# The first pair of inner blocks of the SwiGLU: seven-product scheme against plain products by token halves

## Chip, cores and metric

The kernel runs on one core of one Trainium2 chip. The time is device microseconds (us) of one execution. Engines are named as in the profile: PE is TensorE (PEld its weight loads), DVE is VectorE, ACT is ScalarE, POOL is GpSimd, SP is the engine that issues most DMAs (SPq is its queue). L12 is line 12 of the kernel. All instructions that go through the kernel's recording wrapper carry line L195, so they are told apart here by the names of the tiles they write and read.

## What is computed

One inference step of a two-layer encoder on 576 tokens (512 prompt tokens and 64 of a sample), width 1024. In each layer three mixers, then a cross attention, then a SwiGLU; each adds to the residual `x`. Only the last part and the norm ahead of it matter here:

```python
x = x + mixers(rmsnorm(x, g_mix_norm))
x = x + memory_cross_attention(rmsnorm(x, g_cross_norm), mem_k, mem_v, w)
h = rmsnorm(x, g_ffn_norm)                            # 576 x 1024
x = x + (silu(h @ w_gate) * (h @ w_up)) @ w_down      # inner width 2816
```

## The kernel before

The residual lies transposed in the tile `X`: eight pieces `k` of 128 rows, 576 token columns, in two token halves `a` of HF = 288. Products are made in fp32r with each operand split into a rounded part H and a remainder L (`split_to`, L453: ACT copies H, DVE subtracts to get L), and three matmuls H·H, H·L, L·H per piece (`mm3`, L429). One such matmul is 128x128 by 128x288.

The inner width of 2816 is done in 11 blocks `p` of 256 columns. A block is a gate product and an up product (`gated`, L1658), each from a 1 MB weight slice fetched by SP. Each product is a 2x2 block product (two halves of the 1024 rows, two halves of the output columns, two token halves) that `winograd` (L606) makes with seven products of 12 matmuls where the plain way has eight. For this it needs sums of weight quarters (`wino_w`, L571: four DVE sums and the splits, tiles `sum`, `sH`, `sL`, `wH`, `wL`) and sums of activation quarters. Results come as pairs that ACT and DVE add up (`part` on ACT, then a DVE addition into `gate` or `u`).

The activation quarters come from `WNorm` (L514). `add` (L522) is called after each of the 16 additions into X at the end of cross attention; ACT copies X times the gain into `xs` and squares it, DVE sums the squares (tiles `u`). When a token half `a` is complete, `finish(a)` (L531) has PE sum the squares over rows by a matmul with `ones_x` into a bank T, ACT takes Ln and Exp of it, DVE scales `xs` by the result. For `a` = 0 the two quarters b11, b21 are split into `bH`, `bL`; these are the operands of products 1 and 2. For `a` = 1 DVE and ACT also make t1 = b12-b11, t2 = b22-t1, t3 = b22-b12, t4 = b21-t2 (tiles `tA`, `tB`) and split them and b22 into five tiles `bT`, the operands of products 3 to 7.

Products 1 and 2 of both gate and up of block 0 need nothing of the second token half. `gated` therefore starts gate (`next(g)`) and up (`next(h)`) of block 0 before it runs on with either. All engines' queues are in order; a scheduler sets the order by its own estimates from the order in the code and the data each instruction needs. PSUM banks are three rings, D and T of three and S of two. Raw weights have two slots (`wraw`), and the big tiles (`xs`, `bH`, `bT`, `actH` and others) eleven slots.

Of the kernel before, what the change touches and what calls it, by code (L numbers as in the profile page):

```python
# [25 lines left out]
HF = T // 2  # L26
# [190 lines left out]
def tile_hybrid(ctx, tc, ins, outs):  # L217
# [54 lines left out]
    def ps_(tag):  # L272
        return clock.tile(pp.tile([128, 512], F32, tag=tag, name=nm(tag), bufs=PB[tag]), tag, PB[tag])
# [27 lines left out]
    def tt(out, a, b, op, eng=None):  # L301
        (eng or nc.vector).tensor_tensor(out, a, b, op=op)
# [95 lines left out]
    def load_w(src, kt, n, src2=None, by="m"):  # L398
        return split_w(fetch_w(src, kt, n, src2), by)
# [114 lines left out]
    class WNorm:  # L514
# [16 lines left out]
        def finish(self, a):  # L531

            r = u()[:, 0:HF]
            rstd_bcast(self.acc[a], ones_x, r)
            n = 4 * HF
            b11, b21, b12, b22 = (self.x[i][:, q * n:(q + 1) * n] for i in range(2) for q in range(2))

            def scaled(x):
                x = x.rearrange("p (k t) -> p k t", t=HF)
                tt(x, x, r.unsqueeze(1).broadcast_to([128, 4, HF]), MUL)  # L540

            if a == 0:
# [12 lines left out]
            tt(t2, b22, t1, SUB)
            split_to(t2, Ha[:, n:2 * n], La[:, n:2 * n])
            split_to(t1, Ha[:, 0:n], La[:, 0:n])
            tt(t3, b22, b12, SUB)
            split_to(t3, Hb[:, 0:n], Lb[:, 0:n])
            tt(t4, b21, t2, SUB)  # L560
            split_to(t4, Hb[:, n:2 * n], Lb[:, n:2 * n])
            split_to(b22, Q[:, 0:n], Q[:, n:2 * n])
            self.p.update({5: (Ha, La, 0), 6: (Ha, La, 1), 7: (Hb, Lb, 0), 4: (Hb, Lb, 1), 3: (Q, Q, 0)})

        def part(self, p, i, k):

# [331 lines left out]
    def layer(l, xn):  # L898
# [759 lines left out]
        def gated(p, aH, aL, k0):  # L1658

            cs = lambda a: slice(a * HF, (a + 1) * HF)  # L1660
            done, done2 = [0, 0], [0, 0]
            s = [u("gate") for _ in range(2)]

            def gate(m, a, d, c):
                tt(s[m][:, cs(a)], d, c, ADD)
                done[m] += 1
                if done[m] == 2:
                    act(s[m], s[m], AF.Silu)

# [12 lines left out]

            h = winograd(wino_w(I["w_up"][l, :, p * 256:(p + 1) * 256]), xf, up_)
            next(h)
            if not p:

                run(g)
            run(h)
# [84 lines left out]
```

## Time and profile before

| | |
|---|---|
| median of 3 runs | 1718.99 us (1717.65 to 1723.28) |
| profiled execution, its own time | 1715.83 us |
| its span, first to last instruction | 1714.1 us |
| mean granted TensorE clock | 0.990 of full speed |
| busy: PE, PEld, DVE, ACT, POOL | 96%, 89%, 72%, 53%, 12% |

The busy shares are means over the whole span. A PE instruction counts as busy also while its clock is granted at half rate, so the granted clock and the number of instructions in a stretch are read beside them. Times below are counted from the span's start. The SwiGLU of layer 0 begins at 459 us, that of layer 1 at about 1303.6 us.

### The profile page before, as it was taken

To read this page: it belongs to the slowest core of one execution; us is meant where nothing else is said; L and a number is where in the kernel's file an instruction comes from. 1 tells how busy PE (TensorE), PEld (TensorE's weight loads), DVE (VectorE), ACT (ScalarE), POOL (GpSimd) and SP (SyncE) were. 2 spreads that over 40 slices of the span, in tenths; PEclk is the share of its full clock that TensorE was granted. 3 is DMA by queue.
4 is the path that set the end of the run, shared out by engine and by line. 5 is a ranking of instruction groups with operands and counts; after the bars stand their busy time and mean duration, and the time that the engine had idled before them with its cause. 6 is when DMAs were issued, how large, how long until landed. Compare 5 with 4: busy or idle time off the path is not lost.

```text
span 1714.1 us, 30856 instructions
## 1 busy us (share of the span) xinstructions
PE 1650.6 (96%) x12231; PEld 1532.3 (89%) x12231; DVE 1231.7 (72%) x2496; ACT 904.7 (53%) x1929; POOL 206.7 (12%) x303
## 2 busy tenths in 40 slices
PE   8999989999899999999999989999997999999998
PEld 8887887789889999999998978877897999999998
DVE  5737798776898677766557378987668986766763
ACT  6426678655654444344443456876567544334431
POOL 4323341020000000000134042400200000000000
PEclk9999999999999999999999999999999999999999
DMA  5321230022022323322222213200211233233221
GB/s 165 112 72 58 68 112 26 26 74 75 25 75 98 99 75 98 95 81 96 79 84 84 85 43 105 74 26 25 99 50 50 75 99 99 74 99 99 78 96 56
DMA packets 113647, 133.30 MB, mean 78 GB/s; under 512 B 10610, under 2 KB 95712, under 8 KB 113504
## 3 DMA queue, kind: packets, MB, share of 16 engines
q1 hardware_dynamic: 113120, 131.30, 24.1%
q8 instruction: 96, 1.57, 0.4%
q14 instruction: 47, 0.39, 0.1%
q0 software_dynamic: 352, 0.03, 0.0%
q10 hardware_dynamic: 32, 0.01, 0.0%
HBM read 123.64 MB, written 7.68 MB: 77 GB/s over the span
## 4 chain that ended last, share of the span: by engine, by line
PE 75%; DVE 13%; ACT 4%; issue 3%; POOL 2%; DMA 1%; POOLq 0%; ACTq 0%; DVEq 0%; SPq 0%
PE ffn0.D L195 9%; PE ffn1.D L195 8%; PE ffn0.S L195 6%; PE ffn0.T L195 6%; PE ffn1.S L195 6%; PE ffn1.T L195 6%; PE win1.D L195 4%; PE win0.D L195 4%; PE cross1.D L195 3%; PE cross0.D L195 3%; PE wout1.D L195 2%; PE wout0.D L195 2%; PE cross1.T L195 1%; PE cross0.T L195 1%; PE mlap1.T L195 1%
## 5 line engine op out<-in xcount | busy, mean ns | idle before, releaser
L195 ACT ACTIVATE ffn1.wH<-ffn1.wraw 128x1024 fp32r<-128x1024 f32 x66 | 60.6, 918 | 115.7 <-PE ffn1.T L195 61.4
L195 ACT ACTIVATE ffn0.wH<-ffn0.wraw 128x1024 fp32r<-128x1024 f32 x66 | 60.6, 918 | 111.0 <-PE ffn0.T L195 60.8
L195 DVE TENSOR_TENSOR ffn0.sL<-ffn0.sum,ffn0.sH 128x1024 fp32r<-128x1024 f32 x44 | 53.8, 1222 | 41.1 <-ACT ffn0.sH L195 41.1
L195 DVE TENSOR_TENSOR ffn1.sL<-ffn1.sum,ffn1.sH 128x1024 fp32r<-128x1024 f32 x44 | 53.8, 1222 | 40.4 <-ACT ffn1.sH L195 40.4
L195 PE MATMUL ffn0.D<-cross0.bT,ffn0.sH 128*128 128x288 f32 x352 | 73.9, 301 | 1.5 <-ACT ffn0.sH L195 0.7
L195 PE MATMUL ffn1.D<-cross1.bT,ffn1.sH 128*128 128x288 f32 x352 | 72.8, 297 | 2.2 <-ACT cross1.bT L195 1.2
L195 DVE TENSOR_TENSOR ffn1.wL<-ffn1.wraw,ffn1.wH 128x1024 fp32r<-128x1024 f32 x66 | 68.8, 1044 | 7.8 <-ACT ffn1.wH L195 7.2
L195 DVE TENSOR_TENSOR ffn0.wL<-ffn0.wraw,ffn0.wH 128x1024 fp32r<-128x1024 f32 x66 | 68.8, 1044 | 7.8 <-ACT ffn0.wH L195 7.2
L195 PE MATMUL ffn1.S<-cross1.bT,ffn1.sH 128*128 128x288 f32 x352 | 72.9, 298 | 1.3 <-ACT cross1.bT L195 0.6
L195 PE MATMUL ffn0.S<-cross0.bT,ffn0.sH 128*128 128x288 f32 x352 | 72.9, 298 | 0.7 <-ACT cross0.bT L195 0.5
L195 POOL TENSOR_TENSOR ffn0.u<-ffn0.u,ffn0.u 128x576 f32<-128x576 f32 x6 | 10.0, 1665 | 470.5 <-DVE ffn0.wL L195 463.5
L195 PEld LDWEIGHTS ffn0.D<-cross0.bT,ffn0.sH 128*128 128x128 f32 x352 | 57.6, 192 | 3.7 <-ACT ffn0.part L195 1.2
L195 ACT ACTIVATE ffn0.sH<-ffn0.sum 128x1024 fp32r<-128x1024 f32 x44 | 46.3, 1055 | 27.6 <-PE ffn0.S L195 22.8
L195 ACT ACTIVATE ffn1.sH<-ffn1.sum 128x1024 fp32r<-128x1024 f32 x44 | 46.3, 1055 | 27.4 <-PE ffn1.S L195 23.1
L195 PEld LDWEIGHTS ffn1.D<-cross1.bT,ffn1.sH 128*128 128x128 f32 x352 | 57.1, 190 | 3.6 <-ACT cross1.bT L195 1.4
L195 PEld LDWEIGHTS ffn1.S<-cross1.bT,ffn1.sH 128*128 128x128 f32 x352 | 57.8, 192 | 2.0 <-ACT cross1.bT L195 0.9
L195 PEld LDWEIGHTS ffn0.S<-cross0.bT,ffn0.sH 128*128 128x128 f32 x352 | 57.8, 192 | 1.5 <-ACT cross0.bT L195 0.8
L195 PE MATMUL ffn0.D<-cross0.bT,ffn0.sL 128*128 128x288 f32 x176 | 52.9, 301 | 0.0
L195 PE MATMUL ffn0.S<-cross0.bT,ffn0.sL 128*128 128x288 f32 x176 | 52.8, 300 | 0.0
L195 PE MATMUL ffn1.S<-cross1.bT,ffn1.sL 128*128 128x288 f32 x176 | 52.7, 299 | 0.0
L195 PE MATMUL ffn1.D<-cross1.bT,ffn1.sL 128*128 128x288 f32 x176 | 52.5, 298 | 0.0
L195 ACT ACTIVATE ffn0.part<-ffn0.D 128x288 f32<-128x288 f32 x66 | 26.9, 407 | 41.4 <-PE ffn0.D L195 41.4
(903 smaller groups left out, 6453.9 us busy)
## 6 DMA issues: line engine op xcount, KB each, us to landing
ffn0.wraw<-in_w_gate_dram SPq DMA_DIRECT2D x11, 1024.0 KB, 5.3
ffn0.wraw<-in_w_up_dram SPq DMA_DIRECT2D x11, 1024.0 KB, 5.3
ffn0.wraw<-in_w_down_dram SPq DMA_DIRECT2D x11, 1024.0 KB, 5.0
ffn1.wraw<-in_w_gate_dram SPq DMA_DIRECT2D x11, 1024.0 KB, 5.3
ffn1.wraw<-in_w_up_dram SPq DMA_DIRECT2D x11, 1024.0 KB, 5.4
ffn1.wraw<-in_w_down_dram SPq DMA_DIRECT2D x11, 1024.0 KB, 5.1
win1.wraw<-in_w_in_dram SPq DMA_DIRECT2D x7, 1024.0 KB, 5.4
win0.wraw<-in_w_in_dram SPq DMA_DIRECT2D x6, 1024.0 KB, 5.6
```

The source lines that it names most:

```text
L195: r = fn(*args, **kw)
```

## The change

`finish(1)` only scales and splits the two quarters b12 and b22 (tiles `bQ`, called P and Q below). The four sums move into a method of their own, `sums`, which uses one tile instead of two for them. Block 0 is no longer done by `gated` but by `first`: gate and up as plain products, all of token half 0 (from `bH`, `bL`), then `sums`, then all of token half 1 (from P and Q). Silu reads the PSUM bank directly, and so does the multiplication by it. No weight sums are made for this block. Blocks 1 to 10 stay as they were, without the interleaving.

```diff
@@ WNorm.finish, from L545 @@
                 self.p = {1: (H, L, 0), 2: (H, L, 1)}
+                self.sides = [[(H, L, 0), (H, L, 1)]]
                 return
-            ta, tb = big(name="tA"), big(name="tB")
-            t1, t2, t3, t4 = ta[:, 0:n], ta[:, n:2 * n], tb[:, 0:n], tb[:, n:2 * n]
-            Ha, La, Hb, Lb, Q = (big(F32R, "bT") for _ in range(5))
-            scaled(b12)
-            tt(t1, b12, b11, SUB)
-            scaled(b22)
-            tt(t2, b22, t1, SUB)
-            split_to(t2, Ha[:, n:2 * n], La[:, n:2 * n])
-            split_to(t1, Ha[:, 0:n], La[:, 0:n])
-            tt(t3, b22, b12, SUB)
-            split_to(t3, Hb[:, 0:n], Lb[:, 0:n])
-            tt(t4, b21, t2, SUB)
-            split_to(t4, Hb[:, n:2 * n], Lb[:, n:2 * n])
-            split_to(b22, Q[:, 0:n], Q[:, n:2 * n])
-            self.p.update({5: (Ha, La, 0), 6: (Ha, La, 1), 7: (Hb, Lb, 0), 4: (Hb, Lb, 1), 3: (Q, Q, 0)})
+            P, Q = big(F32R, "bQ"), big(F32R, "bQ")
+            for x, y in ((b12, P), (b22, Q)):
+                scaled(x)
+                split_to(x, y[:, 0:n], y[:, n:2 * n])
+            self.p[3] = (Q, Q, 0)
+            self.sides.append([(P, P, 0), (Q, Q, 0)])
+
+        def sums(self):
...
+            t = big(name="tA")
+            x, y = t[:, 0:n], t[:, n:2 * n]
+            Ha, La, Hb, Lb = (big(F32R, "bT") for _ in range(4))
+            tt(x, b12, b11, SUB)
+            tt(y, b22, x, SUB)
+            split_to(y, Ha[:, n:2 * n], La[:, n:2 * n])
+            split_to(x, Ha[:, 0:n], La[:, 0:n])
+            tt(x, b22, b12, SUB)
+            split_to(x, Hb[:, 0:n], Lb[:, 0:n])
+            tt(y, b21, y, SUB)
+            split_to(y, Hb[:, n:2 * n], Lb[:, n:2 * n])
...
@@ gated, from L1670 @@
-            g = winograd(wino_w(I["w_gate"][l, :, p * 256:(p + 1) * 256]), xf, gate)
-            next(g)
-            if p:
-                run(g)
+            run(winograd(wino_w(I["w_gate"][l, :, p * 256:(p + 1) * 256]), xf, gate))
...
+        def first(aH, aL):
+
+            ws = [load_w(I["w_gate"][l, :, 0:256], KD, 256), None]
+            raw = fetch_w(I["w_up"][l, :, 0:256], KD, 256)
...
+            s, t = [u("gate") for _ in range(2)], [u() for _ in range(2)]
+            n = 0
+            for a in range(2):
+                cs = slice(a * HF, (a + 1) * HF)
+                for w, up_ in zip(ws, (False, True)):
+                    for m in range(2):
+                        d = ps_("DTS"[n % 3])[:, 0:HF]
+                        n += 1
+                        for k in range(KD):
+                            mm3(d, w[0](k, m * 128, m * 128 + 128), w[1](k, m * 128, m * 128 + 128),
+                                xf.plain(a, 0, k), xf.plain(a, 1, k), k == 0, k == KD - 1)
+                        if up_:
+                            tt(t[m][:, cs], d, s[m][:, cs], MUL)
+                        else:
+                            act(s[m][:, cs], d, AF.Silu)
+                        if up_ and a:
+                            split_to(t[m], aH[:, m, :], aL[:, m, :])
+                if not a:
+                    xf.sums()
...
-                gated(p0 + i, aH, aL, 2 * i)
+                if p0 + i:
+                    gated(p0 + i, aH, aL, 2 * i)
+                else:
+                    first(aH, aL)
```

PE's queue of layer 0 around the matmul with `ones_x` for the second token half (T_5585), before:

```order
L195 MATMUL ffn0.D_5699<-cross0.bL_5482,ffn0.wH_5677 128x288
L195 MATMUL ffn0.D_5699<-cross0.bH_5481,ffn0.wL_5678 128x288
L195 MATMUL cross0.T_5585<-cross0.u_5581,ones_x 128x288
L195 MATMUL ffn0.T_5659<-cross0.bH_5481,ffn0.wH_5622 128x288
L195 MATMUL ffn0.T_5659<-cross0.bL_5482,ffn0.wH_5622 128x288
```

and now (S_5680 is an up product of half 0, T_5654 a gate product of half 0):

```order
L195 MATMUL ffn0.S_5680<-cross0.bL_5482,ffn0.sH_5615 128x288
L195 MATMUL ffn0.S_5680<-cross0.bH_5481,ffn0.sL_5616 128x288
L195 MATMUL cross0.T_5585<-cross0.u_5581,ones_x 128x288
L195 MATMUL ffn0.T_5654<-cross0.bH_5481,ffn0.wH_5609 128x288
L195 MATMUL ffn0.T_5654<-cross0.bL_5482,ffn0.wH_5609 128x288
```

Before, 24 matmuls of the SwiGLU stand ahead of T_5585 and 24 that need only the first half behind it; now 46 stand ahead and 50 behind. After those 50 come the 96 of half 1, which read `bQ`.

DVE's queue of layer 0 from the scaling of the second token half on, before:

```order
L195 TENSOR_TENSOR cross0.xs_4717<-cross0.xs_4717,cross0.u_5584 128x1152 x2
L195 TENSOR_TENSOR cross0.tA_5589<-cross0.xs_4717,cross0.xs_4716 128x1152
L195 TENSOR_TENSOR ffn0.gate_5618<-ffn0.T_5659,ffn0.part_5657 128x288
L195 TENSOR_TENSOR cross0.tA_5589<-cross0.xs_4717,cross0.tA_5589 128x1152
L195 TENSOR_TENSOR ffn0.wL_5696<-ffn0.wraw_5675,ffn0.wH_5695 128x512
L195 TENSOR_TENSOR cross0.bT_5592<-cross0.tA_5589,cross0.bT_5591 128x1152 x2
```

and now:

```order
L195 TENSOR_TENSOR cross0.xs_4717<-cross0.xs_4717,cross0.u_5584 128x1152 x2
L195 TENSOR_TENSOR cross0.bQ_5589<-cross0.xs_4717,cross0.bQ_5589 128x1152
L195 TENSOR_TENSOR ffn0.u_5625<-ffn0.S_5680,ffn0.gate_5623 128x288
L195 TENSOR_TENSOR cross0.bQ_5590<-cross0.xs_4717,cross0.bQ_5590 128x1152
L195 TENSOR_TENSOR ffn0.tA_5732<-cross0.xs_4717,cross0.xs_4716 128x1152
L195 TENSOR_TENSOR ffn0.u_5626<-ffn0.D_5706,ffn0.gate_5624 128x288
L195 TENSOR_TENSOR ffn0.tA_5732<-cross0.xs_4717,ffn0.tA_5732 128x1152
L195 TENSOR_TENSOR ffn0.bT_5734<-ffn0.tA_5732,ffn0.bT_5733 128x1152 x2
```

The remainders of P and Q now come ahead of the sums, which follow them.

DVE's queue of layer 0 during the last additions into X of the first token half, before (`wraw_5675` is the up weight of block 0):

```order
L195 TENSOR_TENSOR ffn0.wL_5641<-ffn0.wraw_5620,ffn0.wH_5640 128x512
L195 TENSOR_TENSOR X<-X,cross0.D_5404 128x288
L195 TENSOR_TENSOR cross0.u_5401<-cross0.u_5401,cross0.u_5383 128x288
L195 TENSOR_TENSOR ffn0.sum_5681<-ffn0.wraw_5675 128x512
L195 TENSOR_TENSOR X<-X,cross0.D_5422 128x288
```

and now (`wraw_5861` is the gate weight of block 1, whose DMA takes the slot of block 0's up weight):

```order
L195 TENSOR_TENSOR ffn0.wL_5610<-ffn0.wraw_5603,ffn0.wH_5609 128x1024
L195 TENSOR_TENSOR cross0.u_5401<-cross0.u_5401,cross0.u_5383 128x288
L195 TENSOR_TENSOR X<-X,cross0.D_5404 128x288
L195 TENSOR_TENSOR ffn0.sum_5867<-ffn0.wraw_5861 128x512
L195 TENSOR_TENSOR X<-X,cross0.D_5422 128x288
```

The first reader of the third 1 MB weight slice of the SwiGLU now stands ahead of the addition D_5422 and all later ones into X; before, it was the first reader of the second slice.

## Rows read from the trace of the kernel before

**Rows 1.** Page, part 1: busy us, share of span, instructions.

```profile
PE 1650.6 (96%) x12231; PEld 1532.3 (89%) x12231; DVE 1231.7 (72%) x2496; ACT 904.7 (53%) x1929; POOL 206.7 (12%) x303
```

**Rows 2.** Chain of waits within 620 to 626: start us, us, what.

```profile
622.67 3.19 PE ffn0.D L195 x24
```

**Rows 3.** Windows of 62 us: length, busy us (xinstructions) per engine, PE clock, DMA.

```profile
458.00:520.00 62.00, 54.29 (x353) 51.16 (x352) 54.56 (x73) 37.82 (x58) 0.00 (x0) 0.92 0.21 69
520.00:582.00 62.00, 62.00 (x470) 62.00 (x469) 51.67 (x83) 28.70 (x41) 0.00 (x0) 1.00 0.27 86
1302.50:1364.50 62.00, 52.90 (x353) 49.80 (x352) 54.72 (x73) 37.93 (x58) 0.00 (x0) 0.94 0.21 69
1364.50:1426.50 62.00, 62.00 (x470) 62.00 (x469) 51.58 (x83) 28.90 (x41) 0.00 (x0) 1.00 0.27 86
```

**Rows 4.** Waits of PE, 458 to 496: waited for, us in total, times, longest.

```profile
PE cross0.T L195 <- DVE cross0.u L195: 3.3, 1, 3.3
...
PE ffn0.D L195 <- DVE cross0.bL L195: 0.9, 1, 0.9
...
PE ffn0.D L195 <- ACT cross0.bH L195: 0.3, 1, 0.3
PE ffn0.T L195 <- ACT cross0.bT L195: 0.3, 1, 0.3
```

**Rows 5.** Windows, shorter, the start of layer 0's SwiGLU (columns as in rows 3).

```profile
458.00:464.00 6.00, 4.48 (x30) 3.78 (x28) 6.00 (x10) 5.91 (x13) 0.00 (x0) 1.00 0.01 3
...
467.00:471.00 4.00, 4.00 (x19) 3.90 (x20) 2.34 (x2) 2.87 (x4) 0.00 (x0) 0.62 0.00 0
...
474.00:482.00 8.00, 6.64 (x24) 5.77 (x24) 7.19 (x7) 3.25 (x4) 0.00 (x0) 0.57 0.42 131
```

**Rows 6.** Timeline of PE: start us, us, instruction, shapes [idle before, releaser].

```profile
459.01 0.53 PE L195 MATMUL ffn0.D<-cross0.bH,ffn0.wH 128*128 128x288 f32 x2 [0.25 <-ACT cross0.bH L195]
460.40 0.40 PE L195 MATMUL ffn0.D<-cross0.bL,ffn0.wH 128*128 128x288 f32 x1 [0.86 <-DVE cross0.bL L195]
...
466.86 0.75 PE L195 MATMUL cross0.T<-cross0.u,ones_x 128*128 128x288 f32 x2 [3.26 <-DVE cross0.u L195]
...
468.95 0.45 PE L195 MATMUL ffn0.T<-cross0.bH,ffn0.wL 128*128 128x288 f32 x1
469.19 0.45 PE L195 MATMUL ffn0.T<-cross0.bH,ffn0.wH 128*128 128x288 f32 x1
```

**Rows 7.** Timeline of ACT, 457 to 474.

```profile
457.79 1.17 ACT L195 ACTIVATE cross0.bH<-cross0.xs 128x1152 fp32r<-128x1152 f32 x1 [0.86 <-DVE cross0.xs L195]
...
462.29 0.39 ACT L195 ACTIVATE ffn0.part<-ffn0.D 128x288 f32<-128x288 f32 x1
...
463.63 0.41 ACT L195 ACTIVATE ffn0.part<-ffn0.D 128x288 f32<-128x288 f32 x1
...
468.18 0.45 ACT L195 ACTIVATE cross0.u<-cross0.u 128x288 f32<-128x288 f32 x1
468.64 1.28 ACT L195 ACT_TABLE_LOAD   x1
469.94 0.63 ACT L195 ACTIVATE ffn0.wH<-ffn0.wraw 128x512 fp32r<-128x512 f32 x1
```

**Rows 8.** Timeline of DVE, 455 to 488.

```profile
466.34 0.46 DVE L195 TENSOR_TENSOR cross0.u<-cross0.u,cross0.u 128x288 f32<-128x288 f32 x1 [0.30 <-ACT cross0.u L195]
468.66 2.63 DVE L195 TENSOR_TENSOR cross0.xs<-cross0.xs,cross0.u 128x1152 f32<-128x1152 f32 x2 [1.86 <-ACT cross0.u L195]
471.20 1.35 DVE L195 TENSOR_TENSOR cross0.tA<-cross0.xs,cross0.xs 128x1152 f32<-128x1152 f32 x1
...
474.10 0.68 DVE L195 TENSOR_TENSOR ffn0.wL<-ffn0.wraw,ffn0.wH 128x512 fp32r<-128x512 f32 x1
...
482.40 1.23 DVE L195 TENSOR_TENSOR ffn0.sL<-ffn0.sum,ffn0.sH 128x1024 fp32r<-128x1024 f32 x1 [1.22 <-ACT ffn0.sH L195]
```

**Rows 9.** Page, part 6: DMA issues, KB each, median us from issue to landing.

```profile
ffn0.wraw<-in_w_gate_dram SPq DMA_DIRECT2D x11, 1024.0 KB, 5.3
```

More of the change, by code (lines that the diff above doesn't have):

```diff
@@ L547, in finish, with plain @@
                 self.p = {1: (H, L, 0), 2: (H, L, 1)}
+                self.sides = [[(H, L, 0), (H, L, 1)]]
                 return
-            ta, tb = big(name="tA"), big(name="tB")
-            t1, t2, t3, t4 = ta[:, 0:n], ta[:, n:2 * n], tb[:, 0:n], tb[:, n:2 * n]
-            Ha, La, Hb, Lb, Q = (big(F32R, "bT") for _ in range(5))
-            scaled(b12)
-            tt(t1, b12, b11, SUB)
-            scaled(b22)
-            tt(t2, b22, t1, SUB)
-            split_to(t2, Ha[:, n:2 * n], La[:, n:2 * n])
-            split_to(t1, Ha[:, 0:n], La[:, 0:n])
-            tt(t3, b22, b12, SUB)
-            split_to(t3, Hb[:, 0:n], Lb[:, 0:n])
-            tt(t4, b21, t2, SUB)
-            split_to(t4, Hb[:, n:2 * n], Lb[:, n:2 * n])
-            split_to(b22, Q[:, 0:n], Q[:, n:2 * n])
-            self.p.update({5: (Ha, La, 0), 6: (Ha, La, 1), 7: (Hb, Lb, 0), 4: (Hb, Lb, 1), 3: (Q, Q, 0)})
+            P, Q = big(F32R, "bQ"), big(F32R, "bQ")
[5 more added lines that the diff above has]
+        def sums(self):
+            n = 4 * HF
+            b11, b21, b12, b22 = (self.x[i][:, q * n:(q + 1) * n] for i in range(2) for q in range(2))
+            t = big(name="tA")
[9 more added lines that the diff above has]
+            split_to(y, Hb[:, n:2 * n], Lb[:, n:2 * n])
+            self.p.update({5: (Ha, La, 0), 6: (Ha, La, 1), 7: (Hb, Lb, 0), 4: (Hb, Lb, 1)})
+        def plain(self, a, i, k):
+            t = self.sides[a][k // 4]
+            c = ((t[2] + (i if t[0] is t[1] else 0)) * 4 + k % 4) * HF
+            return t[i][:, c:c + HF]
         def part(self, p, i, k):
@@ L1681, in up_ @@
                     split_to(t[m], aH[:, k0 + m, :], aL[:, k0 + m, :])
[L1683 to L1688, printed above, removed]
+            run(winograd(wino_w(I["w_up"][l, :, p * 256:(p + 1) * 256]), xf, up_))
+        def first(aH, aL):
+            ws = [load_w(I["w_gate"][l, :, 0:256], KD, 256), None]
+            raw = fetch_w(I["w_up"][l, :, 0:256], KD, 256)
+            parts = []
+            for m in range(2):
+                H, L = (clock.tile(turn["pool"].tile([128, 1024], F32R, tag=tag, name=nm(tag), bufs=2), tag, 2)
+                        .rearrange("p (k n) -> p k n", n=128) for tag in ("sH", "sL"))
+                split_to(raw[:, :, m * 128:(m + 1) * 128], H, L)
+                parts.append((H, L))
+            ws[1] = [lambda k, c0, c1, i=i: parts[c0 // 128][i][:, k, :] for i in range(2)]
+            s, t = [u("gate") for _ in range(2)], [u() for _ in range(2)]
[3 more added lines that the diff above has]
+                for w, up_ in zip(ws, (False, True)):
+                    for m in range(2):
+                        d = ps_("DTS"[n % 3])[:, 0:HF]
[11 more added lines that the diff above has]
+                    xf.sums()
         def down(gi, p0, kt, aH, aL):
```

## The prediction

> **What bounds the kernel now.** The page's first part comes first: PE is busy 96% of the span [rows 1], so the change can only win where PE stands or runs slowly. The chain of waits gives PE's pace in the SwiGLU: 24 matmuls of 288 columns in 3.19 us, 0.133 us each [rows 2]. The windows view then shows where this pace is missed. A stretch of 62 us in the middle of the SwiGLU holds 470 PE instructions; the 62 us around its start hold 353, in both layers alike [rows 3]. That is 117 x 0.133 = 15.6 us lost per layer, 31.1 in both, and all of it lies in the stretch that the change rewrites.
>
> The loss has two sources. PE waits eight times, from 3.3 us down to 0.3 [rows 4]. The longest wait is for the sum of squares of the second token half: everything that could run on the first half alone and stood ahead of the matmul with ones_x is used up, and that matmul blocks PE's queue until 466.86 [rows 6]. The later waits are for the sums' H and L parts (bT). The second source is the clock: 1.00 while PE worked up to 464, then a granted 0.62 and 0.57 of full speed in stretches behind the long wait [rows 5]; between 468.95 and 469.19 one matmul takes 0.24 us, the 1.2 GHz level in place of 2.4 [rows 6].
>
> **The change, part by part** (times are layer 0's; layer 1 has the same rows and the same loss).
>
> Added work: eight products for seven, 12 more matmuls for gate and 12 for up. 24 x 0.133 = 3.2 us per layer, on PE, with nothing to hide them: 6.4 us in all.
>
> The long wait. 46 matmuls now stand ahead of the ones_x matmul, three of them before L of the first half is there. From 460.40 [rows 6] the other 43 take 5.7 us, to 466.1. Its input is the last sum of squares, at 466.34 + 0.46 = 466.8 before [rows 8]. ACT's queue paces that sum, and the two part copies of 0.39 and 0.41 us that stood in it [rows 7] are gone, so it comes 0.7 us sooner (both overlap their neighbours a little), at 466.1. The wait goes from 3.3 us to between 0 and 0.7 (0.7 if the copies did not matter); I take 0.2, since the two ends meet.
>
> Does half 1 find its operands? PE: the ones_x matmul takes 0.75 [rows 6], then 50 matmuls of half 0 take 6.7, so half 1 is reached at 473.6. ACT and DVE, all 0.7 earlier than before: Exp, that ended at 468.63 [rows 7], ends at 467.9; the table load of 1.28 to 469.2; Silu of the first gate product, priced as the part copy, 0.4, to 469.6; the H copy of P, as the bH copy, 1.17 [rows 7], to 470.8. DVE scales in 2.63 [rows 8] from 467.95, so the first quarter is there in time and DVE is free at 470.6; L of P takes 1.35, to 472.2. Then on ACT a second Silu and H of Q, to 472.4, on DVE a multiplication of 0.46 and L of Q, to 474.0. PE wants L of P at 473.6 and Q twelve matmuls later, at 475.2. Both are ready, with 1.4 and 1.2 us to spare. I take no wait here; past that slack, a delay costs its own length.
>
> The table load is the one step in that chain that could be longer than its row: 1.28 us, with the next ACT instruction 0.02 us after its end [rows 7]. The Trainium skill (ScalarE: Activation LUTs, What ACT_TABLE_LOAD costs) adds a drain of about 1.38 us to each switch, 2.66 in all; by that P and Q would come 1.4 us later, use up the slack just found and leave up to 0.2 us of wait per layer, 0.4 in the sum. The row shows no such gap, so the sum above goes by the row.
>
> The sums now run on DVE while PE works through half 1, 96 matmuls or 12.8 us, to 486.4; block 1's first two products need only the first half and last 24 matmuls more, to 489.6. DVE from 474.0: four subtractions and four remainders at 1.35, a weight remainder of 0.68, two multiplications of 0.46 and the first weight-sum remainder of 1.23 [rows 8], 13.6 us, plus one H copy of 1.17 that DVE must await: 488.8 if nothing overlaps. Neighbours overlap by nearly 0.1 us each, so about 488. PE wants it at 489.6; slack 1 us or somewhat more. Before, the sums ended at about the same time, but with PE waiting for them. I take no wait here either.
>
> What stays. The wait of 0.3 and 0.9 us for bH and bL [rows 4], and the ones_x matmul, whose 0.75 us is 0.5 more than two rows at the pace: 1.7 us per layer.
>
> What is new in cross attention: on DVE, the first weight sum of block 1 stands ahead of additions into X and needs a DMA that is issued only when block 0's up weight has been split. It lands 5.3 us after issue [rows 9]. DVE has ahead of it, from that split on, eight operations (four additions into X and three sums of squares, 0.46 each, and a remainder of 1.23 [rows 8]), 4.4 us, of which overlaps take some and waits give some back: about 4. So DVE may stand 1.3 us; PE has three D banks to work into meanwhile, and four weight sums, each as long as the 0.68 of a remainder of that size [rows 8], leave DVE's queue in this stretch. Bounds 0 and 1.3 us of delay per layer; I take 0.6, since banks and lighter queue cover part of it. The other DVE and ACT work that goes (the weight sums and their splits) gains nothing more: the windows behind the start are at full pace already [rows 3].
>
> The clock: half 0 and half 1 run without a wait like the one of 3.3 us. The waits of 0.3 and 0.9 us before 464 left it at 1.00 [rows 5]; so I take full speed throughout.
>
> **Sum** per layer: 15.6 regained, less 3.2 for the matmuls, 1.7 that stays, 0.2 and 0.6 for new waits: 9.9 us; 19.8 in both. Against the profiled execution's own 1715.8 that is 1696.0. The median of the runs is 3.2 above it, and the times to come are medians of runs: 1719.0 - 19.8 = **1699.2**. With the unknowns at their good ends (no new waits) 21.4 are gained, which from 1715.8 gives 1694.4; at their bad ends (0.7 and 1.3) 17.4, or 1701.6 from the median.
>
> **The rivals.**
> (1) *A wait takes the place of the one removed.* P and Q, or later the sums, come later than the slack of 1.0 to 1.4 us allows: for it speaks that ACT and DVE are 98% busy or more at the start [rows 5] and that the whole chain hangs on one sum of squares. Against it: DVE and ACT have less to do than before. Two to five us per layer would be given back, the upper end when the clock falls too: gain 10 to 16, 1703 to 1709.
> (2) *Slower: the clock falls and stays down during the pair.* Each matmul at the low level costs 0.24 for 0.133 [rows 6], 0.107 more. All 192 of a layer so: 20.5 us per layer, a gain of 9.9 turned into a loss of 10.6, 1740. From 93 matmuls per layer at the low level on, the change loses. For it: before, the clock was low in most of 467 to 482 [rows 5] although PE did work. Against: it fell only behind the 3.3 us wait, which goes.
> (3) *No change.* The stall is not removed but moves to block 1: if its product 6 waits 8 us or more for the sums, 2 or less of the 9.9 us per layer are left, 4 in both: 1715. For it speaks that the DVE chain of the sums is as long as before and starts 3 us later, behind L of P and of Q; against it, that PE now has 120 matmuls, 16 us, to fill that time.
>
> **How the numbers follow.** Forecast 0.77 (its own range 1694 to 1703), rival (1) 0.15, (2) 0.04, (3) 0.04. The first two are faster by more than 0.3%, or 5.2 us, about what a measurement of this kernel can tell from no change: faster 0.92, same 0.04 from (3), slower 0.04 from (2). The range takes in the forecast's bounds and rival (1), with 2 us below for how single runs lie against the median: 1692 to 1709.
>
> **What would show it.** The 62 us from the same point should hold some 450 PE instructions in place of 353, at a clock of 1.00; the wait for cross0.u should be under 1 us, and no wait for bQ or bT over 1 us should be in the list of PE's waits. One for bQ means rival (1), a clock below 1 without a long wait ahead of it rival (2), a wait for bT or sL of block 1 rival (3). A later start of the SwiGLU, beyond 1 us, would be the weight DMA ahead of the additions into X. The prediction is wrong if the time stays above 1709 or PE's regained instructions do not shorten the span.

## The result, and the profile after

Over four runs each the changed kernel takes 1698.62 us (1695.81 to 1699.62) where the kernel before takes 1719.05 (1717.65 to 1723.28): ratio 0.9874, 95% interval 0.9854 to 0.9895, 20.4 us less. Forecast were 19.8 less and 1699.2. The profiled execution took 1699.62 us, its span 1697.9.

The page's first part: 48 more PE instructions, DVE and ACT lighter, and DVE's busy time 20 us less than in [rows 1].

```profile
PE 1648.0 (97%) x12279; PEld 1534.6 (90%) x12279; DVE 1211.8 (71%) x2462; ACT 898.4 (53%) x1915; POOL 206.6 (12%) x303
```

The windows of the kernel after: 62 us from 1 us ahead of the first product of the SwiGLU in layer 0 and 1 (462.89 and 1297.69 here; rows 3 begin 1 us ahead of 459.01 and 1303.59), and the 62 us behind the first of them (columns as in rows 3).

```profile
461.89:523.89 62.00, 60.61 (x454) 60.04 (x453) 56.22 (x77) 37.83 (x57) 0.00 (x0) 1.00 0.20 62
523.89:585.89 62.00, 62.00 (x470) 62.00 (x469) 47.60 (x76) 27.05 (x39) 0.00 (x0) 1.00 0.29 93
1296.69:1358.69 62.00, 60.63 (x454) 60.05 (x453) 56.23 (x77) 37.83 (x57) 0.00 (x0) 1.00 0.20 62
```

The steady pace is still 470; the stretches at the start hold 454 in both layers where [rows 3] has 353, at a clock of 1.00 instead of 0.92 and 0.94. The stretch that lost 117 x 0.133 = 15.6 us now loses 16 x 0.133 = 2.1 in each layer.

The list of PE's waits from 440 to 530, complete; in [rows 4] it began with 3.3 us for cross0.u.

```profile
PE ffn0.D L195 <- DVE cross0.bL L195: 0.7, 1, 0.7
PE ffn0.D L195 <- ACT cross0.bH L195: 0.7, 1, 0.7
```

PE's timeline: the two starts behind these waits, the matmul with ones_x, the first matmuls of the second token half, and the first that read a sum (block 1).

```profile
462.89 0.40 PE L195 MATMUL ffn0.D<-cross0.bH,ffn0.wH 128*128 128x288 f32 x1 [0.65 <-ACT cross0.bH L195]
464.28 0.40 PE L195 MATMUL ffn0.D<-cross0.bL,ffn0.wH 128*128 128x288 f32 x1 [0.73 <-DVE cross0.bL L195]
...
470.08 0.65 PE L195 MATMUL cross0.T<-cross0.u,ones_x 128*128 128x288 f32 x2
...
477.19 0.43 PE L195 MATMUL ffn0.T<-cross0.bQ,ffn0.wH 128*128 128x288 f32 x2
...
493.12 0.42 PE L195 MATMUL ffn0.D<-ffn0.bT,ffn0.sH 128*128 128x288 f32 x2
```

The chain that makes the second half, on ACT and then on DVE.

```profile
471.76 1.28 ACT L195 ACT_TABLE_LOAD   x1
473.05 0.41 ACT L195 ACTIVATE ffn0.gate<-ffn0.D 128x288 f32<-128x288 f32 x1
```

```profile
471.77 2.63 DVE L195 TENSOR_TENSOR cross0.xs<-cross0.xs,cross0.u 128x1152 f32<-128x1152 f32 x2 [1.92 <-ACT cross0.u L195]
474.55 1.36 DVE L195 TENSOR_TENSOR cross0.bQ<-cross0.xs,cross0.bQ 128x1152 fp32r<-128x1152 f32 x1
...
476.19 1.35 DVE L195 TENSOR_TENSOR cross0.bQ<-cross0.xs,cross0.bQ 128x1152 fp32r<-128x1152 f32 x1
...
489.00 1.22 DVE L195 TENSOR_TENSOR ffn0.sL<-ffn0.sum,ffn0.sH 128x1024 fp32r<-128x1024 f32 x1
```

P's low part is there at 474.55 + 1.36 = 475.91, and PE starts on P at 477.19: 1.3 us to spare, where 1.4 was forecast. The remainder of the weight sum (sL) is there at 489.00 + 1.22 = 490.22, 2.9 us before the first matmul that reads a sum.

### The profile page after: what moved, and what is told of

Its sections match the earlier page's. It is cut to its first block, busy times and chain, and to the rows that moved or that the text cites. A ratio compares the mean times of both kernels' runs of the same rounds, so it can differ in the third digit from the quotient of the medians.

```text
span 1697.9 us, 30894 instructions
## 1 busy us (share of the span) xinstructions
PE 1648.0 (97%) x12279; PEld 1534.6 (90%) x12279; DVE 1211.8 (71%) x2462; ACT 898.4 (53%) x1915; POOL 206.6 (12%) x303
## 4 chain that ended last, share of the span: by engine, by line
PE 77%; DVE 12%; ACT 4%; issue 3%; POOL 2%; DMA 1%; POOLq 0%; ACTq 0%; DVEq 0%; SPq 0%
PE ffn0.D L195 9%; PE ffn1.D L195 9%; PE ffn0.T L195 7%; PE ffn0.S L195 7%; PE ffn1.T L195 7%; PE ffn1.S L195 6%; PE win1.D L195 5%; PE win0.D L195 4%; PE cross0.D L195 3%; PE wout1.D L195 2%; PE wout0.D L195 2%; PE cross1.D L195 2%; PE cross1.T L195 1%; PE cross0.T L195 1%; PE mlap0.T L195 1%
## 5 line engine op out<-in xcount | busy, mean ns | idle before, releaser
L195 PE MATMUL ffn1.D<-ffn1.bT,ffn1.sH 128*128 128x288 f32 x320 | 65.1, 295 | 0.2 <-ACT ffn1.part L195 0.2
L195 PE MATMUL ffn0.D<-ffn0.bT,ffn0.sH 128*128 128x288 f32 x320 | 65.2, 295 | 0.1
L195 PEld LDWEIGHTS ffn1.D<-ffn1.bT,ffn1.sH 128*128 128x128 f32 x320 | 51.6, 189 | 1.0 <-ACT ffn1.part L195 0.9
L195 PEld LDWEIGHTS ffn0.D<-ffn0.bT,ffn0.sH 128*128 128x128 f32 x320 | 51.6, 189 | 0.6 <-ACT ffn0.part L195 0.3
L195 PE MATMUL ffn1.D<-ffn1.bT,ffn1.sL 128*128 128x288 f32 x160 | 47.5, 297 | 0.0
L195 PE MATMUL ffn0.D<-ffn0.bT,ffn0.sL 128*128 128x288 f32 x160 | 47.5, 297 | 0.0
L195 PE MATMUL win1.D<-win1.wH,ffn0.hH 128*128 128x256 f32 (+1 forms) x160 | 47.2, 295 | 0.0
L195 PE MATMUL win0.D<-win0.wH,in.hH 128*128 128x256 f32 (+1 forms) x160 | 46.9, 293 | 0.0
L195 PE MATMUL win0.D<-win0.wL,in.hH 128*128 128x256 f32 (+1 forms) x160 | 45.9, 287 | 0.3 <-DVE win0.wL L195 0.3
L195 PE MATMUL win1.D<-win1.wL,ffn0.hH 128*128 128x256 f32 (+1 forms) x160 | 45.8, 286 | 0.4 <-DVE win1.wL L195 0.4
```

The lines of the kernel that those rows point to most:

```text
L195: r = fn(*args, **kw)
```

## The experiments

Each stands beside the kernel before, run on the same chip. Two measures are used: the median of the runs, and, from one profile, the PE instructions in the 62 us from 1 us ahead of the first product of the SwiGLU in layer 0 and in layer 1. The starts differ by up to 5 us in layer 0 and 14 in layer 1 from kernel to kernel, so each kernel's windows follow its own. Between kernels with the same matmuls, one instruction fewer is 0.133 us lost. Where a time is set against the kernel before, it is against that kernel's median in the same comparison: 1719.35 us for runs 1 to 4, 1720.09 for 5 to 7, 1718.96 for 8 to 10.

| kernel | time, us | ratio to before, 95% | PE in the two windows | longest wait of PE in layer 0's |
|---|---|---|---|---|
| before | 1719.05 | 1 | 353, 353 | 3.3 (cross0.u) |
| after | 1698.62 | 0.9874 (0.9854 to 0.9895) | 454, 454 | 0.7 (bH, bL) |
| after, again | 1698.05 | 0.9874 (0.9859 to 0.9889) | 454, 454 | 0.7 (bH, bL) |
| 1 tile by tile | 1710.25 | 0.9958 (0.9943 to 0.9973) | 413, 418 | 3.4 (bQ) |
| 2 sums first | 1715.54 | 0.9987 (0.9975 to 0.9998) | 389, 392 | 6.1 (bQ) |
| 3 late finish | 1714.96 | 0.9978 (0.9968 to 0.9988) | 374, 364 | 3.4 (bT) |
| 4 24 more matmuls | 1707.37 | 0.9934 (0.9913 to 0.9955) | 453, 454 | 0.7 (bH, bL) |
| 5 finer pieces | 1695.34 | 0.9859 (0.9844 to 0.9873) | 460, 461 | 0.5 (bL) |
| 7 filled waits | 1716.85 | 0.9983 (0.9973 to 0.9992) | 420, 425, 60 of them idle | 1.0 (wH) |
| 8 after, DVE + 1.27 | 1700.44 | 0.9891 (0.9874 to 0.9907) | 451, 451 | 0.7 (bH, bL) |
| 9 after, DVE + 5.1 | 1710.21 | 0.9950 (0.9935 to 0.9964) | 405, 417 | 3.0 (bQ) |
| 10 before, DVE + 3.8 | 1724.96 | 1.0033 (1.0023 to 1.0043) | 336, 332 | 5.9 (wL) |

**1. Plain products, but tile by tile.** Is it the half-first order, or the plain products?

```diff
-            for a in range(2):
-                cs = slice(a * HF, (a + 1) * HF)
-                for w, up_ in zip(ws, (False, True)):
-                    for m in range(2):
+            for w, up_ in zip(ws, (False, True)):
+                for m in range(2):
+                    for a in range(2):
+                        cs = slice(a * HF, (a + 1) * HF)
...
-                if not a:
+                if not up_:
                     xf.sums()
```

> The changed kernel with its plain products taken tile by tile (both token halves of a tile, then the next) instead of half by half, with the sums called after the gate tiles. Same 192 plain products, same work on every engine. Main theory (the order keeps TensorE fed while VectorE and ScalarE make the second half): the first product on P comes some 52 matmuls into the SwiGLU instead of 96, about 471.2 us on the clock of the changed kernel's profile, where ScalarE's copy of P ends at 474.5; a wait of about 3.3 us per layer returns, with up to 3 us of matmuls at half clock behind it: 3.3 to 6 us per layer, time 1705 to 1711. Rival (the plain products and the lighter VectorE and ScalarE work are the gain, not the order): 1697 to 1701, as the changed kernel.

PE's waits of this kernel, 440 to 535:

```profile
PE ffn0.T L195 <- ACT cross0.bQ L195: 3.4, 1, 3.4
...
```

As the main theory has it: a wait of 3.4 us on P, 41 and 36 PE instructions fewer than after (10.2 us), 11.6 us slower. The same plain products in another order give back more than half of the gain. The rest, 9.1 us against the kernel before, they keep.

The wait is as long in layer 1, but what follows it is not the same. PE's timeline, layer 0 and layer 1:

```profile
474.03 0.61 PE L195 MATMUL ffn0.T<-cross0.bQ,ffn0.wH 128*128 128x288 f32 x1 [3.44 <-ACT cross0.bQ L195]
474.44 0.44 PE L195 MATMUL ffn0.D<-cross0.bQ,ffn0.wH 128*128 128x288 f32 x1
474.68 0.44 PE L195 MATMUL ffn0.T<-cross0.bH,ffn0.sH 128*128 128x288 f32 x1
...
1315.46 0.40 PE L195 MATMUL ffn1.T<-cross1.bQ,ffn1.wH 128*128 128x288 f32 x1 [3.44 <-ACT cross1.bQ L195]
1315.70 0.30 PE L195 MATMUL ffn1.D<-cross1.bQ,ffn1.wH 128*128 128x288 f32 x1
1315.83 0.30 PE L195 MATMUL ffn1.T<-cross1.bH,ffn1.sH 128*128 128x288 f32 x1
```

In layer 0 the matmuls behind it are 0.24 us apart (474.44 to 474.68) and the mean clock of the window is 0.97; in layer 1 they are 0.13 apart and it is 1.00. The difference is 5 instructions, 0.7 us.

**2. The sums ahead of P and Q.** Is it needed that the sums stand between the halves?

```diff
-            for x, y in ((b12, P), (b22, Q)):
+            for x in (b12, b22):
                 scaled(x)
+            self.sums()
+            for x, y in ((b12, P), (b22, Q)):
                 split_to(x, y[:, 0:n], y[:, n:2 * n])
```

(and the call between the halves goes)

> The changed kernel with its four sums made ahead of the splits P and Q instead of between the token halves. Same instructions, another order on VectorE and ScalarE. Main theory (VectorE's 8 to 9 us of sums and their splits must not stand between the second half's scaling and its split): P's low part ends at about 485 us instead of 475.9, and it is needed at 477.2; TensorE waits about 8 to 9 us per layer at the start of the second half and runs up to 4 us of matmuls at half clock after it: 9 to 13 us per layer, time 1717 to 1725. Rival (the position of the sums is indifferent, since TensorE has other products to run): 1697 to 1702.

PE's timeline of this kernel, the first matmuls on P, and below it DVE's, the low part of P:

```profile
479.89 0.61 PE L195 MATMUL ffn0.T<-cross0.bQ,ffn0.wH 128*128 128x288 f32 x1 [6.11 <-ACT cross0.bQ L195]
480.29 0.44 PE L195 MATMUL ffn0.S<-cross0.bQ,ffn0.wH 128*128 128x288 f32 x1
480.53 0.44 PE L195 MATMUL ffn0.D<-cross0.bQ,ffn0.sH 128*128 128x288 f32 x1
```

```profile
480.09 1.35 DVE L195 TENSOR_TENSOR cross0.bQ<-cross0.xs,cross0.bQ 128x1152 fp32r<-128x1152 f32 x1
```

The wait is there, 6.1 us where 8 to 9 were expected (P's low part ends at 481.4 instead of 485), behind it matmuls 0.24 us apart (480.29 to 480.53), and 65 and 62 PE instructions fewer than after: 8.6 and 8.2 us per layer, a little under the 9 to 13 expected, 16.9 us on the time. 1715.54 is just below the 1717 to 1725 expected. Nearly all of the gain is gone with the same instructions.

**3. Seven products, the second half's chain called later.** Is the order of PE's queue enough, without plain products?

```diff
-            if step:
+            if step == 1:
                 xf.finish(a)
...
             if not p:
 
+                xf.finish(1)
                 run(g)
```

> The kernel before, seven products as before, with the call that makes the second half (norm and sums) put behind the first two products of gate and of up: 48 matmuls stand ahead of the matmul with ones_x instead of 24. Main theory (with seven products the sums are needed at once after the first 96 matmuls and come no sooner): the wait of 3.3 us for cross0.u goes, the waits for the sums grow by the same; change 0 plus or minus 3 us in the whole: 1716 to 1722. Rival (the order of the queue alone is the gain, plain products aren't needed): both layers gain 6 us or more, 1707 or less.

PE's waits of this kernel, 440 to 535:

```profile
PE ffn0.S L195 <- ACT ffn0.bT L195: 3.4, 1, 3.4
...
PE ffn0.T L195 <- DVE cross0.u L195: 0.5, 1, 0.5
```

The wait for cross0.u falls from 3.3 to 0.5 us and one for the first sum of 3.4 takes its place, as expected. But 4.4 us are gained, a little past the 0 plus or minus 3. A miss in size: 21 and 11 more PE instructions stand in the windows, 2.8 and 1.5 us. Part of it is that the chain ends sooner: the weight remainder of DVE that stood inside it (0.68 us at 474.10, [rows 8]) now runs ahead of it, and the last low part of the chain (of b22) starts 25.3 us after the first product (487.55 - 462.24), 25.8 before (484.82 - 459.01). Where the rest comes from is not told apart. The rival, 6 us or more in each layer, fails.

**4. 24 more matmuls where PE is at its pace.** What do the added matmuls cost?

```diff
         product(x, 1)
+        if again:
+            product(x, 1)
```

(again is true for gate and up of block 5)

> The changed kernel with 24 more matmuls in block 5 of each layer's SwiGLU (the first product of gate and of up is run twice), where TensorE is at its constant pace. Prices the 24 matmuls that the change adds. By the row of 0.133 us each: 3.2 us per layer, 6.4 us in all, 1705.0 (1703.5 to 1706.5). Rival (they are hidden in slack of TensorE's queue): 1697 to 1700.

1707.37 us, 8.8 above the changed kernel and above the 1703.5 to 1706.5 expected; single runs run from 1702.37 to 1709.00, so 6.4 is within the spread and the rival's 1700 is not. From the first product of layer 0's SwiGLU to its last matmul it is 857.44 - 463.09 = 394.35 us against 853.26 - 462.89 = 390.37 in the changed kernel: 4.0 for the expected 3.2, and 4.0 in layer 1 as well. In layer 1 a wait for a copy to SBUF of 1.2 us (at 1546.4), where the changed kernel's longest there is 0.2, makes up the excess; in layer 0 two waits of 0.4 (ones_x) and 0.2 do most of it. That they come from the added matmuls is not shown. The matmuls are not hidden.

**5. The first half in finer pieces.** Can the two waits that are left be had?

```diff
                 for q, x in enumerate((b11, b21)):
-                    scaled(x)
-                    split_to(x, H[:, q * n:(q + 1) * n], L[:, q * n:(q + 1) * n])
+                for q, y in enumerate((b11, b21)):
+                    for c in (0, 2 * HF):
+                        x = y[:, c:c + 2 * HF]
...
+                        split_to(x, H[:, q * n + c:q * n + c + 2 * HF], L[:, q * n + c:q * n + c + 2 * HF])
```

> The changed kernel with the first token half scaled and split in pieces of two of the eight k-slices instead of four. It aims at the two waits that are left at the start of the SwiGLU (0.7 us for bH, 0.7 us for bL) and measures the slack of the chain behind them. If the first products start sooner and nothing else is late: 0.5 to 1.3 us per layer, 1696 to 1698. Rival: the matmul with ones_x needs the last of the additions of squares at about 469.85 us, and TensorE reaches it at 470.08 now; a sooner start turns into a wait there, and the eight smaller VectorE instructions delay that chain further: 0, or up to 1 us worse per layer, 1698 to 1701, with a wait of cross0.T for cross0.u of 0.5 to 1.5 us.

All of PE's waits, 440 to 530, and its first window (its first product is at 459.28):

```profile
PE ffn0.D L195 <- DVE cross0.bL L195: 0.5, 1, 0.5
```

```profile
458.28:520.28 62.00, 61.53 (x460) 61.00 (x459) 57.32 (x81) 38.44 (x59) 0.00 (x0) 1.00 0.19 62
```

One wait of 0.5 us is left of the two, none comes at ones_x, and 460 and 461 PE instructions are the most of any kernel here. 1695.34 us is the lowest median, 2.7 below the changed kernel beside it and just under the 1696 to 1698 expected; the rival, a wait at ones_x, did not come. Its interval and that one's still touch, so the gain over the changed kernel is seen in the waits rather than settled by the times; against the kernel before it is 24.8 us.

**6. The changed kernel again.**

> The changed kernel as it is, once more, beside the others of this call. Ratio to the kernel before as in the first comparison, 0.987 (0.985 to 0.990), and again a span from the first product of layer 0's SwiGLU to its last matmul of about 390 us. If its gain were a matter of that run's half-clock stretches elsewhere in the kernel, that span would come near the 401.6 us of the kernel before.

The ratio is the same, and the span from first product to last matmul is 849.80 - 459.35 = 390.45 us, against 860.62 - 459.01 = 401.61 in the kernel before. The gain is not one run's luck. (This profile's span is 1693.7; why it is 4 us under the first one is told in the last section.)

**7. The waits of the kernel before, filled with idle matmuls.** How much of the 15.6 us is the clock's?

```diff
+            wu = wino_w(I["w_up"][l, :, p * 256:(p + 1) * 256])
...
             next(h)
             if not p:
 
+                d = ps_("S")[:, 0:HF]
+                (H, L), k0 = wu[1]
+                for i in range(FILL):
+                    mm(d, H[:, k0 + i % 4, :], xf.part(1, 0, i % 4), i == 0, i == FILL - 1)
                 run(g)
```

(FILL is 60)

> The kernel before with 60 idle matmuls per layer (into a bank that nothing reads) behind the first products of gate and up: 26 of them stand ahead of the matmul with ones_x and 25 ahead of the first sum, where TensorE waits now. They do no useful work, so this tells the waits from the clock: the waits stay waits (now filled with 60 x 0.133 = 8.0 us of matmuls against waits of 7.7 us), and only the matmuls at half clock (some 41 at 0.24 instead of 0.133 us) can be regained. Theory (part of the 15.6 us is the clock's answer to the waits): about 4 us per layer, 1711 (1708 to 1715). Rival (the clock has no part, all of it is waiting): 1718 to 1722 or slower.

Windows of 5 us in this kernel (columns as in rows 3; its first product is at 461.80, 2.8 us later than before):

```profile
468.00:473.00 5.00, 5.00 (x38) 4.84 (x37) 2.54 (x5) 3.60 (x8) 0.00 (x0) 1.00 0.00 0
473.00:478.00 5.00, 4.11 (x31) 3.88 (x30) 5.00 (x7) 2.58 (x4) 0.00 (x0) 1.00 0.01 2
478.00:483.00 5.00, 4.35 (x19) 4.12 (x20) 5.00 (x5) 2.28 (x3) 0.00 (x0) 0.66 0.67 210
```

and in the kernel before:

```profile
468.00:473.00 5.00, 4.33 (x22) 4.09 (x20) 4.34 (x5) 3.28 (x5) 0.00 (x0) 0.66 0.00 0
473.00:478.00 5.00, 3.42 (x12) 2.66 (x13) 5.00 (x5) 2.39 (x3) 0.00 (x0) 0.68 0.39 117
```

Where the clock was 0.66 and 0.68 it is now 1.00, and one stretch at 0.66 is left, from 478. The two windows of 62 us show how much of the clock came back: 0.97 for 0.92 in layer 0, and all of it, 1.00 for 0.94, in layer 1.

```profile
460.80:522.80 62.00, 59.03 (x420) 57.32 (x418) 55.77 (x75) 39.45 (x59) 0.00 (x0) 0.97 0.22 69
1305.54:1367.54 62.00, 58.42 (x425) 56.57 (x424) 56.36 (x76) 39.35 (x59) 0.00 (x0) 1.00 0.22 69
```

The kernel gained 3.2 us where 8 were expected. Without the 60 idle matmuls the windows hold 360 and 365 instructions, 7 and 12 more than before: 0.9 us, and 1.6 in the layer where no slow matmul is left. My theory that some 4 us per layer are the clock's falls, and 1716.85 lies outside both ranges, next to the rival's. Most of the slow matmuls ran where PE would have waited for the sums anyway: DVE was busy 5.00 of 5 us, and the last low part of its chain starts 25.5 us after the first product (487.32 - 461.80) where it was 25.8. New theory: the chain on DVE and ACT up to the sums sets most of the 15.6 us. Runs 8 to 10 test it.

**8 and 9. DVE delayed ahead of P, in the changed kernel.** Are there really 1.3 us of slack, and what comes past it? One idle subtraction in run 8 (the edit shown), four in run 9 (4 in place of its 1).

```diff
                 scaled(x)
+                for _ in range(1 if y is P else 0):
+                    tt(y[:, n:2 * n], x, x, SUB)
                 split_to(x, y[:, 0:n], y[:, n:2 * n])
```

> The changed kernel with one idle VectorE subtraction of 128x1152 (1.27 us from one start to the next) ahead of the low part of P, in each layer. P's low part then ends at about 477.2 us on the clock of the first profile of the changed kernel, just when TensorE needs it (477.2), and all that VectorE does after it comes 1.27 us later. Theory (the VectorE chain has some 1.3 us of slack at the second token half and about 1 us at the sums): no more than 0.5 us per layer, 1698 to 1699.5. Rival (the chain of VectorE sets the time in the changed kernel too): 1.3 us per layer, 1700.6 or more.

> The same with four such subtractions per layer (5.1 us). By VectorE's order P's low part ends at about 482.9 us instead of 475.9, against a need at 477.2: a wait of about 5.7 us per layer at the second half, no further one at the sums. By the wait alone 11.4 us in both layers, 1709.5; with TensorE at half clock for a while after the wait, as in the experiment that put the sums first (8.6 us lost there with a wait of 6.1), 2 to 2.5 us per layer more, 1714. Range 1708 to 1715. Rival (other products fill the wait): 1702 or less.

Run 8: no new wait in the list, and 451 instructions for 454 in both layers. P's low part ends at 477.2 (475.81 + 1.35), where PE starts on P at 477.05; the row of these first two matmuls is 0.56 us instead of 0.43, so the slack is just used up. By the windows 0.4 us per layer are lost, within the 0.5 expected. By the medians it is 1.8 or 2.4 (against 1698.62 or 1698.05), 1700.44 lies above the 1698 to 1699.5 expected and just under the rival's 1700.6, and the intervals of the ratios overlap. The windows bear the slack out, the times alone do not decide. Run 9, DVE's low part of P:

```profile
482.27 1.35 DVE L195 TENSOR_TENSOR cross0.bQ<-cross0.xs,cross0.bQ 128x1152 fp32r<-128x1152 f32 x1
```

PE's start on P and the matmul that follows it:

```profile
483.68 0.61 PE L195 MATMUL ffn0.T<-cross0.bQ,ffn0.wH 128*128 128x288 f32 x1 [2.99 <-DVE cross0.bQ L195]
484.08 0.44 PE L195 MATMUL ffn0.T<-cross0.bQ,ffn0.wL 128*128 128x288 f32 x1
```

and its windows of 4 us:

```profile
484.00:488.00 4.00, 4.00 (x18) 4.00 (x18) 4.00 (x5) 1.17 (x1) 0.00 (x0) 0.50 0.35 74
488.00:492.00 4.00, 4.00 (x26) 4.00 (x26) 2.76 (x4) 2.42 (x3) 0.00 (x0) 0.79 0.47 193
492.00:496.00 4.00, 4.00 (x32) 4.00 (x31) 3.08 (x4) 2.31 (x4) 0.00 (x0) 1.00 0.00 0
```

PE stood 3.0 us, shorter than the 5.7 expected, since the order put 24 matmuls of block 1 that need only half 0 ahead, and PE came to the remainder of P at 480.5 instead of 477.2. Then the clock was 0.50 and 0.79: 18 and 26 matmuls in 4 us where the last window has 32, 14 + 6 missing, about 2.7 us. 49 and 37 instructions fewer than after make 11.4 us, and 12.2 were measured (against the changed kernel taken again), in the range. In layer 0 wait and slow matmuls together are 5.7 of the 6.5 us lost: here the half clock behind the wait is not hidden.

**10. DVE delayed in the chain of the kernel before.**

```diff
+            for _ in range(3):
+                tt(t2, b12, b12, SUB)
             tt(t2, b22, t1, SUB)
```

> The kernel before with three idle VectorE subtractions of 128x1152 (3 x 1.27 = 3.8 us) in the chain that makes the sums, in each layer. New theory from the run with idle matmuls (full clock, no gain): the 15.6 us are set by the chain on VectorE and ScalarE that ends in the sums; TensorE's half clock lies in its shadow. Then every microsecond on that chain is one on the time: 3.8 per layer (3.3 to 5), 1727.5 (1726 to 1730). Rival (TensorE's own pace, waits and half-clock matmuls, sets the end of this stretch, and the chain has slack): 1721 or less.

PE's waits of this kernel, 440 to 530:

```profile
PE ffn0.D L195 <- DVE ffn0.wL L195: 5.9, 1, 5.9
PE cross0.T L195 <- DVE cross0.u L195: 3.3, 1, 3.3
```

6.0 us slower: 17 and 21 PE instructions fewer in the windows, and 2 and 7 in the 62 us behind them, 6.3 us. The last low part of the chain starts 29.5 us after the first product (487.79 - 458.30), 3.7 later than before. The rival's 1721 or less fails, but 1724.96 is also below the 1726 to 1730 expected: every microsecond on the chain was to be one on the time, and it is 0.8 of one (6.0 of 7.6). The new theory holds in direction, and nearly in size: with the longer chain the order of DVE's queue changed as well (the wait is now for a weight's low part that moved into the chain), so the missing fifth is not told apart.

Behind the wait of 3.3 us for cross0.u, at 466.14, the clock stays at 1.00 here (0.62 in [rows 5]):

```profile
466.00:471.00 5.00, 3.95 (x26) 3.61 (x26) 3.15 (x4) 3.87 (x5) 0.00 (x0) 1.00 0.00 0
```

The 24 matmuls behind it are done 1.5 us sooner after the first product than before (469.79 - 458.30 against 472.03 - 459.01), and the kernel is slower all the same.

## Why the prediction was right

**The 15.6 us.** Right: 117 instructions short became 16. From first product to last matmul the SwiGLU is 11.2 us shorter in layer 0 (401.61 to 390.37) and 10.3 in layer 1 (404.97 to 394.66), 21.5 together, where the sum has 2 x 10.5 (15.6 - 3.2 - 1.7 - 0.2). That they could be regained whole rested on the reading that PE's work on half 0 fills the time of the chain; runs 1 and 2 take that away with the products kept, and lose 11.6 and 16.9 us. One sentence of it was wrong. The prediction called the clock a second source of the loss; run 7 brought the clock back in most of layer 0's stretch and in all of layer 1's, and got 0.9 and 1.6 us. The low clock was mostly in the shadow of the sums. The sum didn't price the clock apart from the waits, so nothing came of it.

That the median lies 0.6 us from the forecast is partly luck: single runs of this kernel spread over 4 us, and the terms are not known that finely.

**24 x 0.133 = 3.2 for the added matmuls.** Right within run 4's 4.0 per layer, which holds waits besides.

**What stays, 1.7.** The waits for bH and bL were 0.7 and 0.7, not 0.3 and 0.9; with the matmul of ones_x (0.65 us, 0.4 over two rows) that is 1.8.

**The wait at ones_x, 0.2 (0 to 0.7).** In the first profile none in layer 0 and 0.2 in layer 1; in the profile taken again 0.3 and none. Right.

**Half 1 finds its operands, 1.4 and 1.2 us to spare.** Measured 1.3 for P. For Q it is the same: its low part ends at 477.54, and twelve matmuls after 477.19 are 478.8. Run 8 spends 1.27 of it without a wait on P. For the table load the row decides again: 471.76 + 1.28 = 473.04, and Silu starts at 473.05. The drain of about 1.38 us that the Trainium skill (ScalarE: Activation LUTs, What ACT_TABLE_LOAD costs) adds to a switch is not in that row either.

**The sums, 1 us or more to spare.** The list of waits has no bT and no sL. Measured are 2.9 us, from the end of sL at 490.22 to the first matmul on a sum at 493.12. In run 8 DVE's order put the last low part of a sum behind sL, where it ends 2.4 us later than in the changed kernel (491.16 for 488.72), still without a wait.

**The delay in cross attention, 0.6 for a DMA (0 to 1.3).** Right in size, only in part right in cause. Counted from 222 us, ahead of anything that the change moves, the SwiGLU starts 0.6 us later in the first profile (462.89 against 459.01, less the 3.25 us by which the same instructions already come later there) and 0.8 in the profile taken again (459.35 against 459.01, and 0.45 by which they come earlier). The DMA is waited for 0.15 us in the first and 0.36 in the second; the longer wait on DVE's way there, 0.66 in both, is one for ACT's copy of the up weight. DVE's timeline of the changed kernel:

```profile
443.62 1.23 DVE L195 TENSOR_TENSOR ffn0.sL<-ffn0.wraw,ffn0.sH 128x1024 fp32r<-128x1024 f32 x1 [0.66 <-ACT ffn0.sH L195]
...
451.60 0.69 DVE L195 TENSOR_TENSOR ffn0.sum<-ffn0.wraw 128x512 f32<-128x512 f32 x1 [0.15 <-DMA ffn0.wraw<-in_w_gate_dram]
```

The addition into X behind the first row, at 444.76, is already 0.7 us late by the same count (440.83 before). That the wait of 0.66 makes most of the 0.6 to 0.8 us is argued from these rows; no run took it away.

**The rivals.** (1) is what runs 1, 2 and 9 make: a wait for bQ, 1710 to 1716, dearer than the 1703 to 1709 given. Two to five microseconds per layer were reckoned, and runs 1, 2 and 9 lose 5.8, 8.5 and 6.1. Their waits are 3.0 to 6.1 us long, and slow matmuls follow in five of the six stretches (the mean clock of the windows is 0.97 and 1.00 in run 1, 0.94 and 0.94 in run 2, 0.94 and 0.97 in run 9). (2) did not come: the clock is 1.00 in both windows. What the prediction held against it, that the clock fell only behind the wait of 3.3 us, is not what the rows of the kernel before show. It was back by 471.50 (matmuls 0.13 us apart), and the stretch at 0.57 from 474 [rows 5] stands behind three shorter waits; PE's timeline:

```profile
473.34 0.40 PE L195 MATMUL ffn0.D<-cross0.bH,ffn0.wH 128*128 128x288 f32 x1 [1.01 <-ACT ffn0.wH L195]
...
474.40 0.40 PE L195 MATMUL ffn0.S<-cross0.bT,ffn0.sH 128*128 128x288 f32 x1 [0.53 <-ACT cross0.bT L195]
475.45 0.61 PE L195 MATMUL ffn0.D<-cross0.bT,ffn0.sH 128*128 128x288 f32 x1 [0.65 <-ACT cross0.bT L195]
```

It cost nothing, since these waits went too. (3) did not come.

## What to carry to other kernels

When the engine that bounds the program stands behind a short chain on other engines, work that needs only what is already there is worth more than its own cost: 3.2 us of added matmuls per layer bought back over 13. It takes both, products that need no sums and the order: the order alone gave 4.4 us (run 3), the plain products in another order 9.1 (run 1) and 3.8 (run 2, against its kernel before), both together 20.4. The operands of the next piece have to stand ahead of the sums that are needed later, on the helping engine too. A low clock beside a wait is a loss only if nothing else is late: fill the wait with idle work once before you count it.

## What the runs showed of the hardware that was not expected

Two profiles of the same changed kernel differ by 4.2 us in span, though layer 0's SwiGLU takes 390.4 us from first product to last matmul in both. Windows from 40 to 60 us, of the kernel before, of the changed kernel, and of the changed kernel again:

```profile
40.00:60.00 20.00, 18.91 (x149) 17.62 (x148) 14.44 (x38) 10.87 (x37) 10.12 (x17) 1.00 0.38 107
```

```profile
40.00:60.00 20.00, 18.90 (x138) 17.61 (x138) 14.26 (x43) 10.70 (x37) 10.36 (x17) 0.92 0.32 91
```

```profile
40.00:60.00 20.00, 18.92 (x150) 17.63 (x149) 14.14 (x42) 11.18 (x39) 10.35 (x17) 1.00 0.31 87
```

In the first profile of the changed kernel the clock is 0.92 and 138 instructions are done, in the other two 1.00 and 149 or 150, with the same work at the same place. From 80 to 100 us it is so once more, here the first profile of the changed kernel and below it the second:

```profile
80.00:100.00 20.00, 17.60 (x122) 14.13 (x122) 13.25 (x20) 4.22 (x10) 13.13 (x11) 0.91 0.26 83
```

```profile
80.00:100.00 20.00, 17.59 (x134) 14.53 (x133) 13.78 (x20) 5.99 (x14) 11.86 (x10) 1.00 0.21 69
```

At 222 us the first profile is 3.7 us behind the second (3.25 + 0.45), most of the 4.2. A stretch at half clock comes in some executions and not in others. So a difference of 3 us between two single profiles of this kernel says nothing, while the count of PE instructions in the stretch that a change touches does. What decides whether such a stretch comes was not tried.

After an idle time of 3.0 us at full clock (run 9) the clock stood at 0.50 in the next 4 us and was back at 1.00 by 492; the two waits of 0.7 us in the changed kernel left it at 1.00. The length of one wait does not settle it: behind the same 3.4 us the matmuls of run 1 are 0.24 us apart in layer 0 and 0.13 in layer 1, behind the same 3.3 us the clock fell to 0.62 in the kernel before and stayed at 1.00 in run 10, and behind waits of 1.0, 0.5 and 0.7 us within 2.1 us it fell to 0.57 [rows 5]. So the slow matmuls that a wait brings differ from case to case here, and what decides it is not shown.
